# The head of a decoder layer: conditioning vector spread by dense matmuls, constant matmuls in between, first k tile as plain fp32 products

## The chip, the core and the metric

The kernel runs on one core of a Trainium2 chip. A core has a matrix engine (TensorE, PE in the profile, with its weight loads as PEld), a vector engine (VectorE, DVE), a scalar engine for activation functions (ScalarE, ACT), GpSimd (POOL) and SyncE (SP), which here only issues DMAs. Each engine works through its own queue in order; semaphores tie the queues together. PE writes to PSUM, from which DVE or ACT fetch the results. The metric is the device time of one execution in microseconds; lower is better.

## The reference

One sequence of 256 tokens, width 2048, goes through one conditioned decoder layer (retention and HGRN2 side by side, then a convolutional feed-forward part) and a last RMSNorm. What matters here is the very start:

```python
mod = jax.nn.silu(c) @ w_ada[l] + b_ada[l]
shift1, scale1, gate1, shift2, scale2, gate2 = jnp.split(mod, 6, axis=-1)
h = modulate(rms_norm(x, g_norm1[l]), shift1, scale1)   # rms_norm(x)*(1+scale1)+shift1
p = h @ w_in[l]
```

`c` is one vector of 2048; `w_ada` is 2048 x 12288, `w_in` 2048 x 12288. All inputs are float32.

## The kernel before

**Layout.** Activations of the first stage stand transposed: `xT` has the 2048 features in 16 k tiles of 128 partitions, 256 tokens along the free dimension. The weights of `h @ w_in` come in 12 groups of 512 columns (`ATT`), each in k tiles of 128 x 512.

**Products.** To keep fp32 accuracy at the rate of the narrower type fp32r, each weight tile is split: `wh` is the tile rounded to fp32r by ACT (`upper`, L167), `wl` the rest, by DVE (`rest`, L172). The activation is split in the same way into a tile `hT` (halves "hi" and "lo"). A product is then three matmuls: hi x wh, lo x wh, hi x wl (`mm_cols`, L212, L213, L216, for groups whose result stays transposed; `mm_rows`, L196, L197, L201, for the others). Without the split, a plain fp32 matmul is one call, which the profile shows as two records.

**Modulation.** `silu(c)` is spread over all partitions as `sc` (128 x 2049, the last column 1 for the bias). `ada_dot` (L420) loads a tile of the transposed `w_ada` in two pieces of 1024 and 1025 columns and has DVE multiply each by `sc` and sum (L426): one dot for each partition. `scale_shift` makes with two such tiles the columns of scale and shift for one k tile (ACT, L437 to L440); `modulated` applies them to x (ACT L350, L354, for k = 0 DVE L352; DVE L355).

**The start, in order.** `constants` (L243) fills the tile `ones`, loads c as two rows on ACT's queue, then `ident` and `gn1`, and spreads c by matmuls with one row of ones against a row of c (L264), into four tiles of PSUM. `norm_x` (L325) loads x in four quarters on SP's queue, squares them (the first on DVE, the others on ACT) and adds each down to 256 columns on DVE; ACT takes Silu of the spread c out of PSUM in between, then switches to the table of Sqrt. `token_rstd` (L295) sums the squares over partitions on PE (L303), takes the root (ACT) and the reciprocal (DVE, L313), and spreads it over partitions by two matmuls with `ident` (L317); `times` (L413) multiplies x by it.

`run` (L760) writes the order of k tiles 0 and 1 by hand: dots of k = 0, then the first 4 groups (`FIRST`) of products with k tile 0, then k tile 1. Two groups stand in two single tiles of PSUM each (`po`, four buffers), two in a double tile (`pg`, two buffers). Up to L827 (`self.ordered = False`) everything that goes through `pin` keeps the program's order on its engine; behind it, the order on ACT, DVE and PE is laid out by a scheduler when the program is built. There the dots of k tile 2 and on run in the background, paced by `pump`; `take` (L790) takes a finished group out of PSUM (ACT L794 for a first part, DVE L796 to add).

**Loads.** All weight tiles share 12 buffers `raw` on SP's queue; a load is issued when its buffer is free and an earlier load has landed.

```python
self.pin(self.nc.sync.dma_start(out=raw, in_=src))
```

Of the kernel before, what the change touches and what calls it, by code (L numbers as in the profile page):

```python
# [19 lines left out]
P = 128  # L20
# [35 lines left out]
class Kernel:  # L56
# [145 lines left out]

    def mm_cols(self, ps, items, first, last):
# [39 lines left out]
    def constants(self):  # L243
# [13 lines left out]
        rows = [self.blk([1, GW], name="crow") for _ in range(2)]  # L257
        for u, row in enumerate(rows):
            nc.scalar.dma_start(out=row, in_=a["c"][:, u * GW : (u + 1) * GW])
        self.small_loads(nc.scalar, ("ident", "gn1"))  # L260
        for u in range(4):
            at = slice(u * G, (u + 1) * G)
            ps = self.po()
            nc.tensor.matmul(ps, lhsT=self.ones[0:1, :], rhs=rows[u // 2][:, u % 2 * G : (u % 2 + 1) * G], start=True, stop=True)  # L264
            self.silu.append((self.sc[:, at], ps))
# [29 lines left out]
    def token_rstd(self, parts):  # L295


        nc = self.nc
        ps = self.po()[:, :NT]
        for i, z in enumerate(parts):  # L300
            for t in range(NT):

                nc.tensor.matmul(  # L303
                    ps[:, t : t + 1],
                    lhsT=z[:, t * P : (t + 1) * P],
                    rhs=self.ones[:, 0:1],
                    start=i == t == 0,
                    stop=i == len(parts) - 1,
                    skip_group_check=True,
                )  # L310
        q = self.small([P, NT], name="rq")
        nc.scalar.activation(q, ps, AF.Sqrt, bias=self.eps1, scale=1.0 / D)
        self.pin(nc.vector.reciprocal(q, q))  # L313

        ps = self.po()[:, :T]
        for t in range(NT):
            nc.tensor.matmul(ps[:, t * P : (t + 1) * P], lhsT=q[:, t : t + 1].to_broadcast([P, P]), rhs=self.ident, start=True, stop=True)  # L317
        return ps
# [6 lines left out]
    def norm_x(self):  # L325
# [4 lines left out]
        for i, x in enumerate(self.xT):  # L330
            z = self.blk([P, 4, T], name="sq")
            if i == 0:
                self.pin(nc.vector.tensor_tensor(z, x, x, ALU.mult))
            else:
                if i < 3:
                    self.pin(nc.scalar.activation(*self.silu.pop(0), AF.Silu))
                self.pin(nc.scalar.activation(z, x, AF.Square))
            self.pin(nc.vector.tensor_tensor(z[:, :2, :], z[:, :2, :], z[:, 2:, :], ALU.add))
            self.pin(nc.vector.tensor_tensor(z[:, 0, :], z[:, 0, :], z[:, 1, :], ALU.add))
            parts.append(z[:, 0, :])  # L340
        for part in self.silu:
            self.pin(nc.scalar.activation(*part, AF.Silu))
# [3 lines left out]
    def modulated(self, dst, x, k, sc, sh):  # L346
# [4 lines left out]
        if k == 0:  # L351
# [68 lines left out]
    def ada_dot(self, src):  # L420

        nc = self.nc
        part = self.small([P, 2], name="dot", bufs=6)
        for u, w in enumerate((GW, D + 1 - GW)):
            raw = self.load(src[:, u * GW : u * GW + w], 1, w)
            dot = self.pin(nc.vector.scalar_tensor_tensor(raw[:, 0, :], raw[:, 0, :], 1.0, self.sc[:, u * GW : u * GW + w], ALU.mult, ALU.mult, accum_out=part[:, u : u + 1]))  # L426
# [5 lines left out]
    def scale_shift(self, name, k, sc, sh, gn):  # L432
# [6 lines left out]
        part = yield from self.ada_dot(self.a[name][k, 1])  # L439
        self.pin(act(sh[:, kk], part[:, 0:1], AF.Identity, bias=part[:, 1:2]))  # L440

# [318 lines left out]
    def run(self):  # L760
# [15 lines left out]
        def ada1(k):  # L776
# [3 lines left out]
            yield from self.scale_shift("ada1", k, s1, t1, self.gn1)  # L780
            if k % 2 == 0:
                hT[k // 2] = self.blk([P, 2, 2 * T], F32R, name="hT")
            self.modulated(act(k), self.xT[k // 4][:, k % 4, :], k, s1, t1)
# [16 lines left out]
        for _ in range(3):  # L800
            next(ada[0])
        rx = self.token_rstd(parts)
        rx_sb = c.tile([P, T], F32, name="rx_sb")
        ps = [self.po2(), self.po2(), self.pg(), self.pg()][:FIRST]
        for k in range(2):
            for i in range(4 if k else 1):
                if k and i == 1:
                    self.times(k, 1, rx)
                next(ada[k])
            if k == 0:  # L810
                self.times(k, 1, rx)

            ahead = 2 * k
            uppers = [self.upper(a["wa"][g][:, k : k + 1, :], 1, G) for g in range(ahead + 1)]
            rests = [self.rest(z) for z in uppers[:ahead]]
            for _ in ada[k]:
                pass
            for g in range(FIRST):
                if g >= ahead:
                    rests.append(self.rest(uppers[g] if g < len(uppers) else self.upper(a["wa"][g][:, k : k + 1, :], 1, G)))  # L820
                wh, wl = rests[g]
                if k == g == 0:
                    self.pin(nc.scalar.activation(rx_sb, rx, AF.Copy))
                mms[g](ps[g], [(act(k), wh[:, 0, :], wl[:, 0, :])], k == 0, k == 1 and g >= RESIDENT)
# [377 lines left out]
def _arrays(x, c, positions, w_ada, b_ada, g_norm1, w_in, w_ret_o, w_hg_o, w_out, hg_lb, g_norm2, w_up, conv_w, conv_b, w_down, g_final):  # L1202
# [4 lines left out]
        "c": c.reshape(1, D),  # L1207
# [45 lines left out]
```

## Time and profile before

| | us |
|---|---|
| median of 3 runs | 1513.63 (1513.56 to 1513.67) |
| the profiled execution | 1513.78 |
| its span, first to last instruction | 1512.0 |
| PE busy in the span | 1496.0 |
| DVE busy | 1206.4 |
| ACT busy | 846.6 |

Times in the rows of the timeline are counted from the start of the span: start, duration, engine, line of the kernel, operation, tiles (written from read), shape and count; in brackets stands how long the engine was idle before and what ended that. Rows of several instructions merge a run of like ones. PE's records end later than the next one starts, since matmuls are pipelined; the rate is read from starts. In the view of windows each row is a stretch: its length, then for PE, PEld, DVE, ACT and POOL the busy time with the number of instructions, PE's granted clock, the DMA share and GB/s. The column of the granted clock shows 1.00 for the whole head; that PE works at half rate there is seen in the spacing of its records alone.

### The profile page before, as it was taken

The numbers are of one execution on the slowest core, as the hardware profiler recorded it, in microseconds if no ns is written. First come the engines' busy times: TensorE is split into PE (matmuls) and PEld (weight loads), VectorE is DVE, ScalarE is ACT, GpSimd is POOL, SyncE is SP. The second block draws the span as 40 slices with busy tenths as digits, with TensorE's granted clock in tenths as the row PEclk, the third lists the DMA queues.
The fourth block names the chain that finished last, engine by engine and source line by source line (L and its number), as shares of the span: only waits on it lengthen the run. The fifth ranks groups of instructions, "written<-read, shape, count | busy, mean of one in ns | idle before, by whom it ended". The sixth has DMA issues, their size and how long they took to land.

```text
span 1512.0 us, 23190 instructions
## 1 busy us (share of the span) xinstructions
PE 1496.0 (99%) x8722; PEld 1288.2 (85%) x8722; DVE 1206.4 (80%) x1639; ACT 846.6 (56%) x1207; POOL 4.0 (0%) x8
## 2 busy tenths in 40 slices
PE   8999999999999999999999999999999999999997
PEld 6999999888888888888888888888888888888886
DVE  7899996997999877898977778778777769455794
ACT  6655454777875644455466555555655558344342
POOL 0000000000000000000000000000000000000000
PEclk9999999999999999999999999999999999999999
DMA  9999997777888889989847777777777766667651
GB/s 374 390 332 340 315 326 230 258 265 251 286 269 289 281 299 326 320 286 362 305 126 244 233 232 230 231 229 236 227 244 230 218 192 204 194 206 214 185 168 56
DMA packets 110996, 385.75 MB, mean 255 GB/s; under 512 B 12802, under 2 KB 13346, under 8 KB 110884
## 3 DMA queue, kind: packets, MB, share of 16 engines
q1 hardware_dynamic: 110016, 383.14, 76.8%
q8 instruction: 68, 1.11, 0.3%
q10 hardware_dynamic: 868, 1.13, 0.2%
q14 instruction: 44, 0.36, 0.1%
HBM read 382.11 MB, written 2.11 MB: 254 GB/s over the span
## 4 chain that ended last, share of the span: by engine, by line
PE 95%; DVE 3%; DMA 1%; ACT 1%; issue 0%; SPq 0%; DVEq 0%; ACTq 0%
PE pg L196 13%; PE pg L197 13%; PE pg L201 13%; PE po L1086 11%; PE pg L1086 10%; PE po L1088 5%; PE pg L1088 5%; PE po L201 3%; PE po L197 3%; PE po L196 3%; PE pg L212 3%; PE pg L213 3%; PE pg L216 3%; PE po L212 1%; PE po L213 1%; PE po L216 1%
## 5 line engine op out<-in xcount | busy, mean ns | idle before, releaser
L167 ACT ACTIVATE wh<-raw 128x1024 fp32r<-128x1024 f32 (+1 forms) x536 | 550.1, 1033 | 514.8 <-PE pg L197 181.1
L172 DVE TENSOR_TENSOR wl<-raw,wh 128x1024 fp32r<-128x1024 f32 (+1 forms) x536 | 634.0, 1189 | 236.0 <-ACT wh L167 232.7
L426 DVE SCALAR_TENSOR_TENSOR raw<-raw,sc 128x1024 f32<-128x1024 f32 x192 | 233.6, 1219 | 0.0
L1086 PE MATMUL po<-h2T,wh 128*128 128x512 f32 x704 | 221.1, 395 | 0.0
L1086 PE MATMUL pg<-h2T,wh 128*128 128x512 f32 x688 | 216.4, 396 | 0.0
L196 PE MATMUL pg<-wh,hT 128*128 128x512 f32 x512 | 202.8, 396 | 0.2 <-ACT p L794 0.2
L197 PE MATMUL pg<-wh,hT 128*128 128x512 f32 x512 | 200.0, 391 | 0.0
L1088 PEld LDWEIGHTS po<-h2T,wl 128*128 128x128 f32 x704 | 132.3, 188 | 31.2
L1088 PEld LDWEIGHTS pg<-h2T,wl 128*128 128x128 f32 x688 | 129.1, 188 | 31.1 <-DVE wl L172 0.5
L1088 PE MATMUL po<-h2T,wl 128*128 128x256 f32 x704 | 138.3, 278 | 0.0
L201 PE MATMUL pg<-wl,hT 128*128 128x512 f32 x512 | 137.4, 390 | 0.0
L1088 PE MATMUL pg<-h2T,wl 128*128 128x256 f32 x688 | 135.3, 278 | 0.1
L201 PEld LDWEIGHTS pg<-wl,hT 128*128 128x128 f32 x512 | 96.0, 188 | 20.4 <-DVE wl L172 0.2
L196 PEld LDWEIGHTS pg<-wh,hT 128*128 128x128 f32 x512 | 96.2, 188 | 19.9 <-ACT p L794 0.4
L197 PEld LDWEIGHTS pg<-wh,hT 128*128 128x128 f32 x512 | 96.2, 188 | 19.1
L1086 PEld LDWEIGHTS po<-h2T,wh 128*128 128x128 f32 x704 | 107.2, 189 | 0.0
L1086 PEld LDWEIGHTS pg<-h2T,wh 128*128 128x128 f32 x688 | 104.7, 189 | 0.0
L212 PE MATMUL pg<-hT,wh 128*128 128x256 f32 x384 | 95.2, 284 | 0.6 <-DVE p L796 0.6
L213 PE MATMUL pg<-hT,wh 128*128 128x256 f32 x384 | 95.1, 284 | 0.0
L212 PEld LDWEIGHTS pg<-hT,wh 128*128 128x128 f32 x384 | 74.1, 193 | 1.1 <-issue 0.8
L213 PEld LDWEIGHTS pg<-hT,wh 128*128 128x128 f32 x384 | 74.0, 193 | 0.3
L197 PE MATMUL pg<-wh,gs 128*128 128x512 f32 x176 | 68.6, 390 | 0.0
(250 smaller groups left out, 2062.7 us busy)
## 6 DMA issues: line engine op xcount, KB each, us to landing
raw<-in_wup SPq DMA_DIRECT2D x176, 512.0 KB, 4.4
raw<-in_wdown SPq DMA_DIRECT2D x88, 512.0 KB, 4.3
raw<-in_wa SPq DMA_DIRECT2D x80, 512.0 KB, 5.7
raw<-in_ada SPq DMA_DIRECT2D x64, 512.5 KB, 5.8
raw<-in_ada SPq DMA_DIRECT2D x64, 512.0 KB, 5.6
raw<-in_wab SPq DMA_DIRECT2D x64, 512.0 KB, 4.9
raw<-in_gate SPq DMA_DIRECT2D x32, 512.5 KB, 4.2
raw<-in_wb SPq DMA_DIRECT2D x32, 512.0 KB, 4.7
```

The source lines that it names most:

```text
L167: self.pin(self.nc.scalar.activation(wh, raw, AF.Copy))
L172: self.last = self.nc.vector.tensor_tensor(wl, raw, wh.bitcast(F32), ALU.subtract)
L196: nc.tensor.matmul(ps[t], lhsT=act[:, hi], rhs=wh, start=first and i == 0, stop=False)
L197: nc.tensor.matmul(ps[t], lhsT=act[:, lo], rhs=wh, start=False, stop=False)
L201: nc.tensor.matmul(ps[t], lhsT=act[:, hi], rhs=wl, start=False, stop=last and i == len(items) - 1)
L212: nc.tensor.matmul(outs[j], lhsT=wh[:, cs[j]], rhs=act[:, :T], start=opens, stop=False, skip_group_check=True)
L213: nc.tensor.matmul(outs[j], lhsT=wh[:, cs[j]], rhs=act[:, T:], start=False, stop=False, skip_group_check=True)
L216: nc.tensor.matmul(outs[j], lhsT=wl[:, cs[j]], rhs=act[:, :T], start=False, stop=last and i == len(items) - 1, skip_group_check=True)
L426: dot = self.pin(nc.vector.scalar_tensor_tensor(raw[:, 0, :], raw[:, 0, :], 1.0, self.sc[:, u * GW : u * GW + w], ALU.mult, ALU.mult, accu ...
L1086: self.pin(nc.tensor.matmul(ps[j + z], lhsT=wh[:, cs[z]], rhs=act, start=kt == 0, stop=False, skip_group_check=bool(begun)))
L1088: nc.tensor.matmul(ps[j + z][:, :T], lhsT=wl[:, cs[z]], rhs=act[:, :T], start=False, stop=kt == KT - 1, skip_group_check=bool(begun))
```

## The change

Four parts, all ahead of the steady products.

1. c is loaded as 128 x 16 columns instead of two rows, ACT takes Silu of it there, and PE spreads it by 16 fp32 matmuls of a column, broadcast to 128 x 128, against `ident`. The four tiles of PSUM are then copied to `sc`, two by ACT, two by DVE. The last quarter of x is squared half by ACT and half by DVE, and goes to the sums as two parts.
2. `idle(n)` issues n fp32 matmuls of `ones` by `ones` whose result nobody reads: 5 ahead of the spread, 4 behind the sums of squares, 8 behind the spread of the reciprocal. The matmuls of this stage are pinned to program order.
3. k tile 0 of the first four groups is computed as plain fp32 products of the raw weight tile and the unsplit h (`mm_plain`), opening the sums in PSUM; the split halves of h for k tile 0, which later groups need, are made behind the first group of k tile 1.
4. The second piece of the dots for the shift of k tiles 0 and 1 is cut in two (`fine`), with one more addition on ACT; loads of k tile 1's dots and of k tile 0's weights alternate on SP's queue.

```diff
+    def mm_plain(self, ps, w, h):
+
+        for j in range(4):
+            out = ps[j // 2][:, j % 2 * T : (j % 2 + 1) * T]
+            self.pin(self.nc.tensor.matmul(out, lhsT=w[:, j * P : (j + 1) * P], rhs=h, start=j % 2 == 0, stop=False, skip_group_check=True))
...
-        rows = [self.blk([1, GW], name="crow") for _ in range(2)]
-        for u, row in enumerate(rows):
-            nc.scalar.dma_start(out=row, in_=a["c"][:, u * GW : (u + 1) * GW])
-        self.small_loads(nc.scalar, ("ident", "gn1"))
+        self.small_loads(nc.scalar, ("c", "ident"))
+        self.pin(nc.scalar.activation(self.c, self.c, AF.Silu))
+        self.small_loads(nc.scalar, ("gn1",))
+        self.idle(5)
         for u in range(4):
-            at = slice(u * G, (u + 1) * G)
             ps = self.po()
-            nc.tensor.matmul(ps, lhsT=self.ones[0:1, :], rhs=rows[u // 2][:, u % 2 * G : (u % 2 + 1) * G], start=True, stop=True)
-            self.silu.append((self.sc[:, at], ps))
+            for i in range(4):
+                k = 4 * u + i
+                self.pin(nc.tensor.matmul(ps[:, i * P : (i + 1) * P], lhsT=self.c[:, k : k + 1].to_broadcast([P, P]), rhs=self.ident, start=True, stop=True))
+            self.silu.append((self.sc[:, u * G : (u + 1) * G], ps))
+
+    def idle(self, n):
+
+        ps = self.pg()[0]
+        for _ in range(n):
+            self.pin(self.nc.tensor.matmul(ps[:, :P], lhsT=self.ones, rhs=self.ones, start=True, stop=True))
...
+        self.idle(4)
+        yield 0.0
         q = self.small([P, NT], name="rq")
         nc.scalar.activation(q, ps, AF.Sqrt, bias=self.eps1, scale=1.0 / D)
         self.pin(nc.vector.reciprocal(q, q))
...
-            nc.tensor.matmul(ps[:, t * P : (t + 1) * P], lhsT=q[:, t : t + 1].to_broadcast([P, P]), rhs=self.ident, start=True, stop=True)
-        return ps
+            self.pin(nc.tensor.matmul(ps[:, t * P : (t + 1) * P], lhsT=q[:, t : t + 1].to_broadcast([P, P]), rhs=self.ident, start=True, stop=True))
+        self.idle(8)
+        yield ps
...
             if i == 0:
+                self.pin(nc.scalar.activation(*self.silu[0], AF.Copy))
                 self.pin(nc.vector.tensor_tensor(z, x, x, ALU.mult))
+            elif i < 3:
+                self.pin(nc.scalar.activation(z, x, AF.Square))
             else:
-                if i < 3:
-                    self.pin(nc.scalar.activation(*self.silu.pop(0), AF.Silu))
-                self.pin(nc.scalar.activation(z, x, AF.Square))
+                self.pin(nc.scalar.activation(z[:, :2, :], x[:, :2, :], AF.Square))
+                self.pin(nc.vector.tensor_tensor(z[:, 2:, :], x[:, 2:, :], x[:, 2:, :], ALU.mult))
             self.pin(nc.vector.tensor_tensor(z[:, :2, :], z[:, :2, :], z[:, 2:, :], ALU.add))
-            self.pin(nc.vector.tensor_tensor(z[:, 0, :], z[:, 0, :], z[:, 1, :], ALU.add))
+            if i < 3:
+                self.pin(nc.vector.tensor_tensor(z[:, 0, :], z[:, 0, :], z[:, 1, :], ALU.add))
+            else:
+                parts.append(z[:, 1, :])
+            if i in (1, 2):
+                self.pin(nc.vector.tensor_copy(*self.silu[i]))
             parts.append(z[:, 0, :])
-        for part in self.silu:
-            self.pin(nc.scalar.activation(*part, AF.Silu))
+        self.pin(nc.scalar.activation(*self.silu[3], AF.Copy))
...
-        part = yield from self.ada_dot(self.a[name][k, 1])
+        part = yield from self.ada_dot(self.a[name][k, 1], (0, GW, GW + G, D + 1) if fine else (0, GW, D + 1))
         self.pin(act(sh[:, kk], part[:, 0:1], AF.Identity, bias=part[:, 1:2]))
+        if fine:
+            self.pin(act(sh[:, kk], part[:, 2:3], AF.Identity, bias=sh[:, kk]))
...
+        rstd = self.token_rstd(parts)
+        next(rstd)
+        for _ in range(2):
+            next(ada[0])
+        rx = next(rstd)
         rx_sb = c.tile([P, T], F32, name="rx_sb")
+        next(ada[0])
+        self.times(0, 1, rx)
+        for _ in ada[0]:
+            pass
+        h0 = self.s1([P, T], name="h")
+        self.pin(nc.vector.tensor_scalar(h0, self.xT[0][:, 0, :], s1[:, 0:1], t1[:, 0:1], ALU.mult, ALU.add))
+        self.times(1, 1, rx)
         ps = [self.po2(), self.po2(), self.pg(), self.pg()][:FIRST]
...
+        raws = [self.load(a["wa"][0][:, 0:1, :], 1, G)]
+        for g in range(FIRST):
+            next(ada[1])
+            if g + 1 < FIRST:
+                raws.append(self.load(a["wa"][g + 1][:, 0:1, :], 1, G))
+            self.mm_plain(ps[g], raws[g][:, 0, :], h0)
+            if g == 0:
+                self.pin(nc.scalar.activation(rx_sb, rx, AF.Copy))
+        ahead = [self.upper(a["wa"][g][:, 1:2, :], 1, G) for g in range(1)]
+        for _ in ada[1]:
+            pass
+        for g in range(FIRST):
+            wh, wl = self.rest(ahead[g] if g < len(ahead) else self.upper(a["wa"][g][:, 1:2, :], 1, G))
+            mms[g](ps[g], [(act(1), wh[:, 0, :], wl[:, 0, :])], False, g >= RESIDENT)
+            if g == 0:
+                hi, lo = act(0)[:, :T], act(0)[:, T:]
+                self.pin(nc.scalar.activation(hi, h0, AF.Copy))
+                self.pin(nc.vector.tensor_tensor(lo, h0, hi.bitcast(F32), ALU.subtract))
...
-        "c": c.reshape(1, D),
+        "c": cols(c),
```

More of the change, by code (lines that the diff above doesn't have):

```diff
@@ L301, in token_rstd @@
             for t in range(NT):
[L303 to L309, printed above, removed]
-                )
+                self.pin(
+                    nc.tensor.matmul(
+                        ps[:, t : t + 1],
+                        lhsT=z[:, t * P : (t + 1) * P],
+                        rhs=self.ones[:, 0:1],
+                        start=i == t == 0,
+                        stop=i == len(parts) - 1,
+                        skip_group_check=True,
+                    )
+                )
+        self.idle(4)
+        yield 0.0
         q = self.small([P, NT], name="rq")
@@ L350, in modulated @@
         self.pin(act(dst[:, :T], x, AF.Identity, bias=sh[:, k : k + 1], scale=sc[:, k : k + 1]))
-        if k == 0:
+        if k == 1:
             self.pin(self.nc.vector.tensor_scalar(h, x, sc[:, k : k + 1], sh[:, k : k + 1], ALU.mult, ALU.add))
@@ L418, in times, with ada_dot @@
         return ins
-    def ada_dot(self, src):
+    def ada_dot(self, src, cuts=(0, GW, D + 1)):
         nc = self.nc
[L423 to L426, printed above, removed]
+        part = self.small([P, 3], name="dot", bufs=6)
+        for u, (at, to) in enumerate(zip(cuts, cuts[1:])):
+            raw = self.load(src[:, at:to], 1, to - at)
+            dot = self.pin(nc.vector.scalar_tensor_tensor(raw[:, 0, :], raw[:, 0, :], 1.0, self.sc[:, at:to], ALU.mult, ALU.mult, accum_out=part[:, u : u + 1]))
             if not self.ordered:
@@ L430, in ada_dot, with scale_shift @@
         return part
-    def scale_shift(self, name, k, sc, sh, gn):
+    def scale_shift(self, name, k, sc, sh, gn, fine=False):
         act = self.nc.scalar.activation
@@ L779, in ada1 @@
                 self.tc.add_manual_dep(ins.ins, self.last.ins.name, NOSYNC, reason="behind the weights traced ahead of it")
-            yield from self.scale_shift("ada1", k, s1, t1, self.gn1)
+            yield from self.scale_shift("ada1", k, s1, t1, self.gn1, fine=k < 2)
             if k % 2 == 0:
                 hT[k // 2] = self.blk([P, 2, 2 * T], F32R, name="hT")
+            if k == 0:
+                return
             self.modulated(act(k), self.xT[k // 4][:, k % 4, :], k, s1, t1)
@@ L799, in run @@
         ada = [ada1(k) for k in range(KT)]
-        for _ in range(3):
+        rstd = self.token_rstd(parts)
+        next(rstd)
+        for _ in range(2):
             next(ada[0])
-        rx = self.token_rstd(parts)
+        rx = next(rstd)
         rx_sb = c.tile([P, T], F32, name="rx_sb")
-        ps = [self.po2(), self.po2(), self.pg(), self.pg()][:FIRST]
[L805 to L824, printed above, removed]
```

## The prediction

> **What bounds the kernel now.** The page first: the span, the engines' busy time, the shares of the chain that ended last. The profiled execution took 1513.78 us, 1.8 us more than its span; the median of the runs shown is 1513.63 us, so 0.15 us lower.
>
> ```profile
> span 1512.0 us, 23190 instructions
> ...
> PE 1496.0 (99%) x8722; PEld 1288.2 (85%) x8722; DVE 1206.4 (80%) x1639; ACT 846.6 (56%) x1207; POOL 4.0 (0%) x8
> ...
> PE 95%; DVE 3%; DMA 1%; ACT 1%; issue 0%; SPq 0%; DVEq 0%; ACTq 0%
> ```
>
> PE sets the time. So I ask where PE is not full, with the view of windows:
>
> ```profile
> 0.00:16.97 16.97, 11.88 (x28) 6.88 (x28) 11.53 (x26) 10.41 (x17) 0.20 (x4) 1.00 0.90 336
> 16.97:32.56 15.59, 14.51 (x96) 13.89 (x96) 15.17 (x26) 8.70 (x17) 0.00 (x0) 1.00 1.03 406
> 32.56:280.00 247.44, 246.93 (x1758) 233.44 (x1758) 214.17 (x277) 141.66 (x198) 1.91 (x2) 1.00 0.91 318
> ```
>
> From 32.56 us PE is busy 246.93 of 247.44 us. Whatever moves the start of that stretch moves the end of the program by as much; the change can work only on the 32.6 us ahead of it. There the DMA share is 0.90 and then 1.03 (336 and 406 GB/s), and DVE is busy 15.17 of 15.59 us: data and DVE are short there, not PE. The chain of the head says the same:
>
> ```profile
> 2.13 6.48 DMA xT<-in_xT
> ...
> 8.64 1.07 ACT sq L337
> ...
> 10.88 3.55 DVE raw L426 x6
> ...
> 14.56 1.24 PE po L317 x4
> ```
>
> x lands, its last quarter is squared, then come three dots in 3.55 us, 1.18 us each. PE's clock is read from starts in the timeline:
>
> ```profile
> 2.26 7.16 PE L264 MATMUL po<-crow,ones 1*128 1x512 f32 x8 [2.26 <-DMA crow<-in_c]
> ...
> 18.88 1.05 PE L216 MATMUL po<-hT,wl 128*128 128x256 f32 x4
> ...
> 19.74 0.41 PE L212 MATMUL po<-hT,wh 128*128 128x256 f32 x1
> ...
> 22.41 0.64 PE L216 MATMUL pg<-hT,wl 128*128 128x256 f32 x4
> ...
> 22.88 0.28 PE L212 MATMUL pg<-hT,wh 128*128 128x256 f32 x1
> ...
> 466.37 1.02 PE L717 MATMUL po<-p,p 128*128 128x256 f32 x4
> 467.23 0.61 PE L719 MATMUL po<-p,p 128*128 128x128 f32 x4
> ```
>
> At 18.88 four matmuls of 256 columns take 0.86 us from start to start, 0.215 each; at 22.41 0.47 us, 0.12 each. So the clock doubled at about 22 us, 5 us after the first product; 7 us of matmuls with one row (L264) had not opened it. A plain fp32 record of 256 columns takes 0.215 at full clock (L717: 0.86 for four), and one call makes two records.
>
> **The change part by part.** Spread of c and the norm: what the removed and added operations cost.
>
> ```profile
> 1.56 0.39 ACTq L271 DMA_DIRECT2D ident<-in_ident  x1
> ...
> 4.33 0.60 ACT L336 ACTIVATE sc<-po 128x512 f32<-128x512 f32 x1 [0.59 <-PE po L264]
> ...
> 5.86 1.06 ACT L337 ACTIVATE sq<-xT 128x1024 f32<-128x1024 f32 x1 [0.93 <-DMA xT<-in_xT]
> ...
> 9.72 0.69 DVE L338 TENSOR_TENSOR sq<-sq 128x512 f32<-128x512 f32 x1
> ...
> 10.45 0.42 DVE L339 TENSOR_TENSOR sq<-sq 128x256 f32<-128x256 f32 x1
> ...
> 10.79 1.22 DVE L426 SCALAR_TENSOR_TENSOR raw<-raw,sc 128x1024 f32<-128x1024 f32 x1
> ```
>
> ```profile
> ident<-in_ident ACTq DMA_DIRECT2D x1, 64.0 KB, 4.5
> ```
>
> ```profile
> L410 DVE CAST h2T<-h x12: 285/289/295, 775.7 to 789.2; 128x256 fp32r<-128x256 f32 x12
> ```
>
> Before, the spread needed only the row of c (PE starts at 2.26). Now it needs `ident`, which landed at 1.56 + 4.5 = 6.1 us. It moves up by one place on ACT's queue, so it lands between 3.3 (where the five idle matmuls, ten records of about 0.21 from 1.0 us, end) and 6.0; I take 4.8, the row's 6.1 less one quarter of x (512 KB at 406 GB/s, 1.3 us), with which ACT's loads seem to take turns. ACT has a table load, then Silu of 128x16, ahead of that; c is the first load on the queue. At half clock a 128-column fp32 record takes two passes, as long as one pass of 256: 0.215. The first 512 columns are 4 calls, 8 records, 1.7 us, with 0.2 of drain done at 6.7. Now ACT's order counts: Copy (0.60) stands ahead of the first Square (1.06), which was at 5.86; it ends at 8.4 instead of 6.9.
>
> DVE follows, all in program order: add and add (0.69 + 0.42 + gaps = 1.15), copy of 512 columns from PSUM, 1.15, copy, half a square 0.70, one add 0.72. No row shows that copy: a cast of 256 takes 0.285, so 0.57 for 512, and an add of 512 takes 0.69; I take 0.6 (another 0.1 would cost 0.2 in all). Sum: 8.4 + 4.9 = 13.3 us for the first dot, which was at 10.79: **2.5 us later**. The balance of squares between ACT and DVE does not pay for two copies and the wait for the spread.
>
> From dots to the first product:
>
> ```profile
> 14.34 0.16 DVE L313 RECIPROCAL rq<-rq 128x2 f32<-128x2 f32 x1
> ...
> 15.76 0.29 ACT L440 ACTIVATE t<-dot 128x1 f32<-128x1 f32 x1
> 15.82 0.42 DVE L416 TENSOR_TENSOR xT<-xT,po 128x256 f32<-128x256 f32 x1
> ...
> 16.35 0.41 DVE L352 TENSOR_SCALAR h<-xT,s,t 128x256 f32<-128x256 f32 x1
> ...
> 16.98 0.80 PE L212 MATMUL po<-hT,wh 128*128 128x256 f32 x2 [1.20 <-ACT hT L350]
> ...
> 17.30 2.49 DVE L172 TENSOR_TENSOR wl<-raw,wh 128x512 fp32r<-128x512 f32 x4
> ```
>
> Two dots 2.4, reciprocal 0.16, a dot 1.2, `times` 0.44, two half dots 0.68 each (as an add of 512), ACT's last shift 0.3, h0 0.41: 13.3 + 6.35 = 19.65. First product at 19.7 instead of 16.98. The reciprocal needs Sqrt: Copy of the fourth quarter, a table load and Sqrt end near 15, under the second dot. The broadcast (L317) hides under the third dot and the idle(8) (16 records at 0.11, 1.8 us at full clock, 3.4 at half) under what follows; at half clock it would end at 20.3, 0.6 too late. The idle(4) lies in PE's wait for the reciprocal.
>
> Products of k=0: split, 4 groups of 12 matmuls, 48 x 0.12 = 5.76 us at full clock; plain, 16 calls x 2 x 0.215 = 6.9. From 19.7 they end at 26.6, if the clock is open. What goes is four ACT copies and four subtracts, 2.49 us of DVE in this stretch; two more instructions (the halves of act(0)) are moved behind k=1's first group, one each on ACT and DVE (0.4).
>
> ```profile
> 24.62 0.08 DVE L426 DVE_READ_ACCUMULATOR raw<-raw,sc 128x1 f32 x1
> ...
> 25.86 0.75 PE L212 MATMUL po<-hT,wh 128*128 128x256 f32 x4 [0.66 <-ACT hT L350]
> ```
>
> k=1: after h0, DVE has `times` 0.44, three dots 3.6, two half dots 1.36: 25.05, against 24.7 before. The data for the last of them are 7 MB into the stream, as before; at 406 GB/s they are in by about 23, so DVE is last, not DMA. From there to PE was 25.86 - 24.62 = 1.24 us: ready at 26.3. PE is free at 26.6, so PE now comes last, and the 0.66 us wait goes. 5.76 us more: 32.4, with the drain 32.55.
>
> ```profile
> 31.71 0.64 PE L216 MATMUL pg<-hT,wl 128*128 128x256 f32 x4
> ```
>
> Before, this ended at 31.71 + 0.64 = 32.35. **Sum: +0.2 us.** Loads: the same bytes; two pieces of the shifts are halved, two issues more on SP (some 0.35 us each, hidden: SP waits for landings). The plain products keep their four raw buffers until PE has read them, about 22 to 26.6 us, where DVE freed them by 20; eight loads are on the way then, about 6 us of data, which covers it.
>
> What follows stays in place only if ACT lets it:
>
> ```profile
> 30.77 1.22 DVE L172 TENSOR_TENSOR wl<-raw,wh 128x1024 fp32r<-128x1024 f32 x1
> 30.89 0.30 ACT L437 ACTIVATE s<-dot 128x1 f32<-128x1 f32 x1 [0.94 <-DVE raw L426]
> ...
> 31.51 1.01 ACT L794 ACTIVATE p<-pg 128x1024 f32<-128x1024 f32 x1
> ...
> 32.57 0.50 PE L196 MATMUL pg<-wh,hT 128*128 128x512 f32 x1 [0.22 <-ACT p L794]
> ...
> 34.52 1.08 PE L201 MATMUL pg<-wl,hT 128*128 128x512 f32 x4
> ```
>
> PE's next group waits for the eviction p, which stood behind the scale s of k=2, and that for a dot. DVE now ends that dot about 2 us later (25.8 h, 26.3 lo, then four wl, lo of k=0, `times`, two dots: 32.85 against 30.85). This part is not in program order (L827), so p may stand ahead of s in the new program; p then starts at 31 and costs nothing. The next wl ends at 34.1, and PE wants it 1.95 us after 32.6, at 34.55: just in time.
>
> A rule against the row: the Trainium skill, "TensorE: Matmul & The Clock Gate", Part 1, says that only the first 3.4 us or so of matmuls run at half clock, counted in time and not in instructions. Taken alone, it would have opened the clock during L264, and the change would have nothing to win; the row of L264 (7.16 us) and the 0.215 at 18.88 do not agree, so operand rows seem to count.
>
> **The rivals.** 0.2% of the time, 3.0 us, is about what a measurement of this kernel can tell from no change.
>
> *The eviction stays behind the scale.* s at 32.9, two scales 0.65, p 1.0: PE resumes at 34.6, +2.0: 1515.8. For it: that is the order of before. Against: p's group ends 1.9 us ahead of the dot now. Chance 0.22.
>
> *Slower: the clock is shut at the first product.* Place: between the spread and 19.7 PE has only the ten small sums of squares (L303) and 12 idle calls, with gaps up to 1.5 us. Price: idle(8) late by 0.6, and every us at half clock loses 0.5; 5 us, as after 16.98, lose 2.5. With the 0.2: +3.3, 1517.1; if the idle calls count towards those 5 us, +1.9. It is slower by over 3.0 us if the clock comes later than 4.5 us after the first product. For it: the clock of before stayed shut through 1.24 us of L317 and the waits about it. Against: 16 calls of 128 rows are 6.9 us of dense work, more than the 5 that opened it before. Chance 0.17.
>
> *The spread is early.* `ident` at 3.3, or the clock open within the spread, so that the first 512 columns are out 0.9 to 1.5 us sooner. Then the first Square is bound by x's second quarter, the first dot comes at 11.85, the first product at 18.2, k=1 at 25.1: -1.5, 1512.3. The rule of the Trainium skill quoted above would open the clock by about 5 us and give about -0.7. Chance 0.17.
>
> *The whole head gains over 3 us.* k=1 would have to start before 23.2, with its last shift dot done by 22; its data are in at about 23. Only a better order later on could add to -1.5. Chance 0.04.
>
> **How the numbers follow.** Forecast +0.2 us, chance 0.40: 1513.78 + 0.2 = 1514.0 us. Its own range is 1513 to 1515. The range that leaves out 2 in 10 goes from below the early spread (1512.3, less 0.7 for cheaper copies) to just over the shut clock: 1511.6 to 1517.3. Slower by over 0.2%: two thirds of the shut clock, 0.11, and 0.03 for a shut clock and a late eviction together or a worse order later. Faster: 0.04 and 0.02 for the like. Within: 0.80.
>
> **What would show it.** Right: first dot near 13.3, first product near 19.7 at 0.215 per record, k=1 at about 26.6 with no wait for hT, and a dense PE from about 32.6. Wrong: 0.43 per record at the first product (shut clock), p behind s on ACT, `ident` landed by 3.5, or a start of dense PE off by more than 3 us.

## The result, and the profile after

The kernel after the change takes 1517.29 us (median of 11 runs, 1516.98 to 1518.44), the kernel before 1513.67 us beside it (11 runs): a ratio of 1.0024, interval 1.0016 to 1.0031. It is **slower by 3.6 us, 0.24%**. The forecast was +0.2 us with a range of 1511.6 to 1517.3: the time lies at the very edge of the range, and the loss is over the 0.2% that the prediction took as the line between a change and none. The profiled execution took 1517.3 us, 3.5 us more than that of before.

In kernel.py of after, the lines have moved: the spread of c is L271, the constant matmuls L278, the sums of squares L317, the spread of the reciprocal L334, the plain products L207, split products L218, L219, L222, the dots L450, the evictions L822.

The page of after, the two rows that answer to the first fence of the prediction:

```profile
span 1515.5 us, 23278 instructions
...
PE 1498.3 (99%) x8768; PEld 1294.4 (85%) x8768; DVE 1205.9 (80%) x1642; ACT 843.1 (56%) x1203; POOL 4.0 (0%) x8
```

PE is busy 2.3 us more, and the span is 3.5 us longer: PE bounds the time as before, and the stretch in which it is full begins later. The timeline of after, from the loads to k tile 1 (start, duration, engine, line, operation):

```profile
1.17 0.46 ACTq L284 DMA_DIRECT2D ident<-in_ident  x1
...
4.93 0.22 ACT L264 ACTIVATE c<-c 128x16 f32<-128x16 f32 x1 [1.99 <-DMA c<-in_c]
...
6.53 5.85 PE L271 MATMUL po<-ident,c 128*128 128x128 f32 x32 [2.97 <-DMA ident<-in_ident]
...
8.61 0.60 ACT L351 ACTIVATE sc<-po 128x512 f32<-128x512 f32 x1 [3.46 <-PE po L271]
9.11 1.99 ACT L354 ACTIVATE sq<-xT 128x1024 f32<-128x1024 f32 x2
...
14.92 1.22 DVE L450 SCALAR_TENSOR_TENSOR raw<-raw,sc 128x1024 f32<-128x1024 f32 x1
...
18.41 3.21 PE L278 MATMUL pg<-ones 128*128 128x128 f32 x16
...
20.72 0.41 DVE L839 TENSOR_SCALAR h<-xT,s,t 128x256 f32<-128x256 f32 x1 [0.42 <-ACT t L466]
...
21.45 3.62 PE L207 MATMUL po<-h,raw 128*128 128x256 f32 x16
24.91 3.62 PE L207 MATMUL pg<-h,raw 128*128 128x256 f32 x16
28.17 0.58 PE L218 MATMUL po<-hT,wh 128*128 128x256 f32 x2
```

PE waits 2.97 us for `ident` and starts the spread at 6.53. ACT's Copy stands ahead of its first Square and waits for the spread, so the Squares run from 9.11 (before: 5.86) and the first dot from 14.92 (before: 10.79). The first product is at 21.45 (before: 16.98). From there on the change works: the plain products take 6.72 us at full clock, and k tile 1 starts at 28.17 with no wait, where before it had waited 0.66 us at 25.86. So of the 4.5 us by which the first product is late, 2.3 are left at k tile 1. The chain of waits of after names the same path:

```profile
1.17 5.22 DMA ident<-in_ident
...
8.61 0.60 ACT sc L351
...
18.62 3.00 PE pg L278 x16
```

The clock in the head, by the view of windows (after the length of the stretch stands PE's busy time; the granted clock is the first of the last three columns; it shows a shut clock only after the clock had once been open):

```profile
14.00:18.00 4.00, 2.54 (x19) 2.38 (x20) 3.89 (x8) 1.41 (x5) 0.00 (x0) 0.95 1.03 389
18.00:22.00 4.00, 4.00 (x22) 3.95 (x22) 3.42 (x10) 1.02 (x4) 0.00 (x0) 0.62 1.04 403
```

The clock was shut again from about 17.6 us (0.95 of four us: 0.4 us at half rate) to 21.0 (0.62: 3.0 us at half rate), 3.4 us in all. The 16 records of the idle(8) fell into this stretch: they took 3.0 us, from 18.41 to the first product at 21.45. h had been ready at 20.72 + 0.41 = 21.13, so constant work held the first product for 0.3 us.

Behind k tile 1, the timeline of after with PE, ACT and DVE:

```profile
32.87 1.02 ACT L822 ACTIVATE p<-pg 128x1024 f32<-128x1024 f32 x1 [3.84 <-PE pg L222]
...
33.63 0.64 PE L222 MATMUL pg<-hT,wl 128*128 128x256 f32 x4
...
33.79 1.05 ACT L167 ACTIVATE wh<-raw 128x1024 fp32r<-128x1024 f32 x1
...
34.89 0.50 PE L196 MATMUL pg<-wh,hT 128*128 128x512 f32 x1 [0.62 <-ACT wh L167]
...
40.66 1.03 ACT L822 ACTIVATE p<-pg 128x1024 f32<-128x1024 f32 x1 [0.74 <-PE pg L201]
41.58 0.29 ACT L464 ACTIVATE t<-dot 128x1 f32<-128x1 f32 x1
...
43.03 1.22 DVE L450 SCALAR_TENSOR_TENSOR raw<-raw,sc 128x1024 f32<-128x1024 f32 x1
...
44.17 0.42 DVE L379 TENSOR_TENSOR hT<-h,hT 128x256 fp32r<-128x256 f32 x1
...
44.65 0.38 PE L219 MATMUL pg<-hT,wh 128*128 128x256 f32 x1 [1.03 <-DVE hT L379]
```

The rows of before that answer to wh, t and the low half of hT:

```profile
28.88 1.06 ACT L167 ACTIVATE wh<-raw 128x1024 fp32r<-128x1024 f32 x1 [2.06 <-DMA raw<-in_wa]
...
36.56 0.28 ACT L440 ACTIVATE t<-dot 128x1 f32<-128x1 f32 x1
...
40.72 0.42 DVE L355 TENSOR_TENSOR hT<-h,hT 128x256 fp32r<-128x256 f32 x1
```

Two things are new here. First, before, ACT made the split wh of the fifth group (the one that PE needs next) at 28.88, as soon as its data had landed and ahead of the eviction p. In after, the same data landed at 31.2, but ACT stands idle for 3.84 us, until 32.87, in front of the eviction, and wh is queued behind it: PE waits 0.62 us for wh and resumes at 34.89, 2.32 us later than before (32.57). Second, the shift t of k tile 2 now stands behind the eviction of the sixth group (before: of the fifth), 5.0 us later than before, and the low half of hT behind one more dot on DVE: PE waits 1.03 us at 44.65, where before it had no wait.

So the 3.5 us come in three steps. At 34.27, the end of k tile 1's products (before: 32.35), PE is 1.9 us late; the wait of 0.62 against 0.22 makes it 2.32; the wait at k tile 2 makes it 3.45. The same instructions of PE then stand 3.45 to 3.48 us later than before up to the end.

### The profile page after: what moved, and what is told of

It is laid out like the page before. It is cut to its first block, busy times and chain, and to the rows that moved or that the text cites. A ratio compares the mean times of both kernels' runs of the same rounds, so it can differ in the third digit from the quotient of the medians.

```text
span 1515.5 us, 23278 instructions
## 1 busy us (share of the span) xinstructions
PE 1498.3 (99%) x8768; PEld 1294.4 (85%) x8768; DVE 1205.9 (80%) x1642; ACT 843.1 (56%) x1203; POOL 4.0 (0%) x8
## 4 chain that ended last, share of the span: by engine, by line
PE 96%; DVE 2%; DMA 1%; ACT 0%; issue 0%; DVEq 0%; ACTq 0%
PE pg L196 14%; PE pg L197 13%; PE pg L201 13%; PE po L1121 11%; PE pg L1121 10%; PE po L1123 5%; PE pg L1123 5%; PE po L196 3%; PE po L197 3%; PE po L201 3%; PE pg L219 3%; PE pg L218 3%; PE pg L222 3%; PE po L222 1%; PE po L219 1%; PE po L218 1%
## 5 line engine op out<-in xcount | busy, mean ns | idle before, releaser
L450 DVE SCALAR_TENSOR_TENSOR raw<-raw,sc 128x1024 f32<-128x1024 f32 (+2 forms) x194 | 233.9, 1209 | 0.0
L219 PE MATMUL pg<-hT,wh 128*128 128x256 f32 x376 | 92.7, 283 | 1.0 <-DVE hT L379 1.0
L218 PE MATMUL pg<-hT,wh 128*128 128x256 f32 x376 | 92.8, 283 | 0.6 <-DVE p L824 0.6
L219 PEld LDWEIGHTS pg<-hT,wh 128*128 128x128 f32 x376 | 72.1, 192 | 1.4 <-DVE hT L379 1.2
L218 PEld LDWEIGHTS pg<-hT,wh 128*128 128x128 f32 x376 | 72.1, 192 | 1.1 <-issue 0.8
```

The costliest lines, as they stand in the source:

```text
L218: nc.tensor.matmul(outs[j], lhsT=wh[:, cs[j]], rhs=act[:, :T], start=opens, stop=False, skip_group_check=True)
L219: nc.tensor.matmul(outs[j], lhsT=wh[:, cs[j]], rhs=act[:, T:], start=False, stop=False, skip_group_check=True)
```

## The experiments

The theory behind them: the late spread (`ident` as a condition, Copy ahead of Square) costs the head about 3 us, and the order that the scheduler lays out for ACT and DVE behind the edited part costs another 1.5. Rivals: the constant matmuls hold PE up; the plain products hold their buffers, so that loads come late; the blocked SP queue delays the loads of the head. Part 4 of the change (the cut pieces and the alternating loads) stays in all of them and was not tried by itself. Each kernel is the one after, with the edit shown; its time stands beside runs of the kernel before on the same chip (medians 1513.80, 1513.81 and 1514.04 us in the three batches). All differences below are taken against these; after's own is +3.62 us.

### The three parts, one at a time

**The spread of c by rows, as before.** The old spread, the old Silu out of PSUM and the old squares (all four quarters whole); with the dense spread its idle(5) goes too. The idle(4), the idle(8), the plain products and the order of loads stay.

```diff
-        self.small_loads(nc.scalar, ("c", "ident"))
-        self.pin(nc.scalar.activation(self.c, self.c, AF.Silu))
-        self.small_loads(nc.scalar, ("gn1",))
-        self.idle(5)
+        rows = [self.blk([1, GW], name="crow") for _ in range(2)]
...
+            nc.tensor.matmul(ps, lhsT=self.ones[0:1, :], rhs=rows[u // 2][:, u % 2 * G : (u % 2 + 1) * G], start=True, stop=True)
...
+                    self.pin(nc.scalar.activation(*self.silu.pop(0), AF.Silu))
...
```

> The changed kernel with the old spread and the old squares: c as two rows, one-row matmuls, Silu out of PSUM, no five constant matmuls in front; the other constant matmuls, the plain products of k tile 0 and the new order stay. Theory A: first dot at 10.8, reciprocal at 13.3, first product at 17.2 to 17.7 at half clock, k tile 1 from about 25.5, dense PE from about 32.4, time near 1513.5, 3.5 us below the changed kernel. Theory B: dense PE stays behind 34, time over 1516.

Measured: 1514.48 us (1514.33 to 1514.78), +0.68, ratio 1.0004, interval 0.9994 to 1.0013. Its timeline:

```profile
10.73 1.22 DVE L443 SCALAR_TENSOR_TENSOR raw<-raw,sc 128x1024 f32<-128x1024 f32 x1
...
14.72 1.06 PE L333 MATMUL po<-ident,rq 128*128 128x128 f32 x4
...
15.82 0.42 DVE L433 TENSOR_TENSOR xT<-xT,po 128x256 f32<-128x256 f32 x1 [1.18 <-PE po L333]
...
18.36 3.72 PE L207 MATMUL po<-h,raw 128*128 128x256 f32 x16
...
31.90 0.50 PE L196 MATMUL pg<-wh,hT 128*128 128x512 f32 x1 [0.63 <-ACT wh L167]
...
41.67 0.38 PE L219 MATMUL pg<-hT,wh 128*128 128x256 f32 x1 [1.03 <-DVE hT L372]
```

The first dot is back at 10.73, and PE resumes at 31.90 instead of 34.89. The dense spread, with the copies and the divided squares that this run takes back together with it, costs 3.0 us in the trace and 2.9 in the medians. Both later waits (0.63 and 1.03) are still there, so they do not come from the late head: they belong to the order behind it. Spread and order together cost more than the 3.5 us of the loss, since the rest of the change wins: here PE resumes 0.67 us sooner than before (32.57) although it waits 0.4 us longer for wh, so that some 1.1 us are won ahead of it. And the idle(4) at half clock now holds the spread of the reciprocal: DVE waits 1.18 us for it.

**Split products for k tile 0 again.**

```diff
-            self.mm_plain(ps[g], raws[g][:, 0, :], h0)
...
+            mms[g](ps[g], [(act(0), wh[:, 0, :], wl[:, 0, :])], True, False)
```

> The changed kernel with k tile 0 of the first four groups as split products again. If the plain products pay: DVE has four subtracts and the low half (2.9 us) ahead of k tile 1's dots, k tile 1 starts at about 30.3 instead of 28.2, time 1519. If they cost (6.9 us of PE instead of 5.8): k tile 1 starts 1.1 us sooner, time 1516.2.

Measured: 1521.70 us (4 runs, 1519.59 to 1521.85), +7.9, ratio 1.0047, interval 1.0031 to 1.0062. The timeline shows the waits that the plain products had removed:

```profile
22.74 0.39 PE L218 MATMUL po<-hT,wh 128*128 128x256 f32 x1 [0.27 <-ACT wh L167]
...
30.95 0.50 PE L218 MATMUL po<-hT,wh 128*128 128x256 f32 x2 [1.51 <-ACT hT L374]
```

The first product is 1.3 us later than in after, mostly because the clock was shut for longer in this execution (the idle(8) ended at 22.5). k tile 1 waits 1.51 us for hT, since DVE has four subtracts between the dots; and with PE waiting, the clock was shut once more, from 32.4 to 35.8 us (records 0.21 us apart). PE resumes at 39.30, 4.4 us behind after. By the medians the plain products are worth 4.3 us within the change, by the fastest run of each 2.6: more than the roughly 2 us that I had put on them. How much of the 4.3 is the products' own is not shown: the longer shut clock ahead of the first product is in it, and the fastest run has no trace. The theory that they lose time falls.

**Without the constant matmuls.**

```diff
-        self.idle(5)
...
-        self.idle(4)
...
-        self.idle(8)
```

> The changed kernel without its 17 constant matmuls. If they keep the clock open, the first products run at 0.43 us per record for 3 us or more, and the time is 1518.5 to 1520. Theory C (they cost more than they bring: the clock shut at 17.6 us all the same, and the last eight run at half clock in front of the first product): first product 0.2 to 0.3 us sooner, and the time within 0.5 us of 1517.3 if the clock opens in the products as soon as with them.

Measured: 1519.34 us (5 runs, 1518.88 to 1519.7), +5.5, ratio 1.0036, interval 1.0023 to 1.0049. The timeline, for the first half of the plain products:

```profile
20.91 6.56 PE L207 MATMUL po<-h,raw 128*128 128x256 f32 x16 [2.57 <-DVE h L836]
```

and the view of windows:

```profile
26.00:30.00 4.00, 4.00 (x18) 3.43 (x18) 3.51 (x8) 2.71 (x6) 0.00 (x0) 0.91 0.94 328
```

The first product comes 0.54 us sooner (0.36 of that because `ident` landed sooner in this execution: the spread started at 6.17), but its 16 records take 6.4 us from start to start of the next group instead of 3.46: the clock was shut until 26.7 us (0.91 of the four us from 26: 0.7 us at half rate). The constant matmuls together are worth 1.9 us in the medians. They are not the loss.

### Why the head is late

**`c` and `ident` on SP's queue, ahead of x.**

```diff
-        self.small_loads(nc.scalar, ("c", "ident"))
+        self.small_loads(nc.sync, ("c", "ident"))
```

> The changed kernel with one edit: c and ident are loaded by SP's queue ahead of x, not by ACT's beside it. Theory A (late head: the spread waits for ident until 6.5 us, and the squares, copies and dots wait for the spread): ident lands by 3.5 to 4, first dot near 12.2 instead of 14.9, first product near 19 instead of 21.5, dense PE from about 32.5 instead of 34.9, and 1514 to 1515 us instead of 1517.3. Theory B (the end of the head is set behind the products: PE waits for the split of the next group, which ACT does behind an eviction): the head in front moves by 2.5 us, dense PE by under 1 us, time 1516.5 or more.

Measured: 1516.24 us (1515.91 to 1517.24), +2.4, ratio 1.0015, interval 1.0006 to 1.0025. Timeline:

```profile
3.52 4.75 PE L271 MATMUL po<-ident,c 128*128 128x128 f32 x32
...
12.88 1.22 DVE L450 SCALAR_TENSOR_TENSOR raw<-raw,sc 128x1024 f32<-128x1024 f32 x1
...
14.74 2.05 PE L278 MATMUL pg<-ones 128*128 128x128 f32 x8
16.59 1.06 PE L334 MATMUL po<-ident,rq 128*128 128x128 f32 x4
...
17.69 0.42 DVE L440 TENSOR_TENSOR xT<-xT,po 128x256 f32<-128x256 f32 x1 [1.18 <-PE po L334]
...
20.22 3.72 PE L207 MATMUL po<-h,raw 128*128 128x256 f32 x16
```

`ident` landed at 3.39 by the trace, and x paid for it: its first quarter landed at 5.52 instead of 4.73, and ACT waited for the others. So the spread starts 3.0 us sooner and the first dot 2.0, but the first product only 1.2. The clock opened early and was shut again by the time of the last sums: the idle(4) takes 2.05 us, the spread of the reciprocal starts at 16.59 although the reciprocal is done at about 15.4, and DVE waits 1.18 us for it, the same as with the spread by rows. So the late `ident` is a cause, and the idle(4) takes part of what an early `ident` gives. The wait of 0.62 us for wh and that at k tile 2 stayed.

**The same without the idle(4).**

```diff
-        self.idle(4)
```

> The first experiment (c and ident ahead of x, 1516.2) without the four constant matmuls behind the sums of squares. There they ran at half clock, 2.05 us, in front of the spread of the reciprocal, and DVE waited 1.2 us for it. Theory C (in a stretch where the clock is shut a constant matmul costs what it takes): that wait goes; the eight behind it, at half clock 3.4 us from 16.3, then hold the first product at 19.7 instead of 20.2; time 1515.7. If the four keep the clock, it opens one window (3.4 us) later without them and the time rises by up to 1.7 us.

Measured: 1515.56 us (1515.0 to 1516.49), +1.5, ratio 1.0010, interval 1.0000 to 1.0020: 0.9 us less than with it. The spread of the reciprocal is at 15.37 and the first product at 19.49. What is left of the loss is, by the trace, 0.36 us where PE resumes (32.93) and 1.15 at k tile 2.

**`gn1` loaded ahead of the Silu of c.** A load on ACT's queue that waits behind an activation landed at 11.59 us, and SP's queue waited 3.8 us for it.

```diff
-        self.small_loads(nc.scalar, ("c", "ident"))
+        self.small_loads(nc.scalar, ("c", "ident", "gn1"))
         self.pin(nc.scalar.activation(self.c, self.c, AF.Silu))
-        self.small_loads(nc.scalar, ("gn1",))
```

> The changed kernel with gn1 loaded ahead of Silu of c on ACT's queue. In the changed kernel SP's queue stood from 7.8 to 11.6 us for the landing of gn1, and the loads behind it land 1 to 2 us late. If data bind the head, k tile 1 and the next groups come up to 1 us sooner, 1516.3. By theories A and B (dots and order bind) the time stays within 0.3 us of 1517.3.

Measured: 1517.36 us (1517.16 to 1518.41), +3.3, ratio 1.0023, interval 1.0014 to 1.0033. `gn1` landed at 7.76, SP's wait for it fell from 3.8 to 1.0 us, and some loads landed up to 1.1 us sooner; the first product is at 21.30 instead of 21.45, and the time is that of after. In the head of after the loads on SP's queue do not bind; the rival falls.

### The order behind the head

**The split of the fifth group emitted first.** The generator's first step (which splits wh) is taken before the scheduler's part begins.

```diff
+        early = [next(self.pieces(a["wa"][FIRST][:, 0:2, :], 2))]
...
-                    take(g, self.products(mms[g], self.pg(), a["wa"][g], act, done[g], m), done[g] == 0)
+                    take(g, self.products(mms[g], self.pg(), a["wa"][g], act, done[g], m, steps=early), done[g] == 0)
```

> The changed kernel with one edit: the split of the first weight tile of the next group (fifth) is written ahead of the two evictions, in program order. Theory B: ACT does it at about 31.3, when its data land, PE resumes at 33.9 behind the eviction alone instead of 34.9, and the time falls by 0.9 us to 1516.4. Theory A: PE also resumes 0.9 us sooner, but that is all of it; the other 2.6 us stay. If the data bind (landing 31.2), nothing changes.

Measured: 1517.24 us (1517.04 to 1518.63), +3.4, ratio 1.0024, interval 1.0015 to 1.0034. The scheduler still put the eviction ahead of wh, and PE waited the same 0.62 us. The edit did not bring about what it was to test, so this says nothing of the order.

**The order written out by hand.** wh of the fifth group ahead of the evictions, and the rest of k tile 2's dots and halves ahead of the eviction of the sixth group, all pinned; the scheduler's part begins behind it.

```diff
-                    nc.scalar.activation(dst, z, AF.Copy)
+                    self.pin(nc.scalar.activation(dst, z, AF.Copy))
...
+        steps = begun(4, 2)
...
+        z = self.products(mms[4], self.pg(), a["wa"][4], act, 0, 2, steps=steps)
+        steps = begun(5, 2)
+        take(4, z, True)
...
+        six = begun(6, 3)
+        for _ in ada[2]:
+            pass
+        take(5, z, True)
```

> The changed kernel with the order of ACT and DVE written out by hand up to the sixth group: split of the fifth group's tile, evictions of groups three and four, scales of k tile 2, then the rest of k tile 2 ahead of the sixth group's eviction. Theory B (what is left behind the head is order): PE resumes at about 34.3 right behind k tile 1's last product instead of 34.9, the wait of 1.0 us for the low half of k tile 2 goes, together 1.7 us: 1515.6. If the data of these groups bind instead, the wait moves to the next tile and the time stays at 1517.3.

Measured: 1516.79 us (1515.78 to 1517.06), +3.0, ratio 1.0017, interval 1.0008 to 1.0026. ACT's timeline:

```profile
32.13 1.06 ACT L167 ACTIVATE wh<-raw 128x1024 fp32r<-128x1024 f32 x1 [2.16 <-DMA raw<-in_wa]
33.67 1.02 ACT L822 ACTIVATE p<-pg 128x1024 f32<-128x1024 f32 x1 [0.47 <-PE pg L222]
...
40.13 0.29 ACT L464 ACTIVATE t<-dot 128x1 f32<-128x1 f32 x1 [0.30 <-DVE raw L450]
40.45 0.60 ACT L374 ACTIVATE hT<-xT,t,s 128x256 fp32r<-128x256 f32 x1
...
41.45 1.00 ACT L822 ACTIVATE p<-pg 128x1024 f32<-128x1024 f32 x1
```

and further on, in the chain of waits:

```profile
136.43 0.96 ACT wh L167
137.43 0.39 PE pg L218
```

wh now runs while ACT had been idle, and t and hT ahead of the eviction. Both waits of PE are gone, so they were made by the order. PE is 2.3 us late at the start of the dense stretch and stays so past k tile 2. Two things eat into the gain. In this execution the clock was shut from 14.8 to 21.6, and the first product was at 22.22, 0.77 later than in after. And at 137 us a new wait for wh appears (0.46 us), behind which PE is 3.0 us late instead of 2.3.

**Spread by rows and the order by hand together.** The first and the last edit in one kernel.

```diff
+        rows = [self.blk([1, GW], name="crow") for _ in range(2)]
...
+        steps = begun(4, 2)
...
```

> The kernel with the old spread (the third experiment, 1514.5) with the same order by hand. If head and order add up: 1514.5 - 1.7 = 1512.8, 0.9 us below the kernel before. If PE meets its data instead, since the loads of the head run at the same 400 GB/s, it stays at 1513.7 or more.

Measured: 1513.76 us (1513.64 to 1514.45), -0.05, ratio 0.9999, interval 0.9991 to 1.0008. By the trace, PE is 0.6 to 0.75 us ahead of before up to 120 us, and level with it from 134 us on, where it waits for wh (0.46 us). With the two causes taken away together the whole loss is gone; what would have been a gain is given back at 134 us.

### What the parts could bring

**As the last, without the idle(4).**

```diff
-        self.idle(4)
```

> The same without the four constant matmuls behind the sums of squares, which ran at half clock (2 us) in front of the spread of the reciprocal there. The wait of 1.2 us for it ahead of the product with x goes; first product at 17.2 instead of 18.4, k tile 1 bound by its dots and data near 24.6 instead of 25.2: 0.5 us less than the kernel with them, 1512.3. If the clock then opens later, the products of k tile 0 lose up to 1.7 us and nothing is won.

Measured: **1512.90 us** (1512.63 to 1513.96), -0.9, ratio 0.9994, interval 0.9985 to 1.0003. Timeline:

```profile
13.88 1.22 PE L332 MATMUL po<-ident,rq 128*128 128x128 f32 x4 [0.55 <-DVE rq L328]
14.90 3.20 PE L277 MATMUL pg<-ones 128*128 128x128 f32 x16
17.94 3.62 PE L207 MATMUL po<-h,raw 128*128 128x256 f32 x16
```

The spread of the reciprocal now waits for nothing but the reciprocal. The first product is 0.97 us sooner than in the run with the idle(4) and runs at full clock all the same: the idle(4) was of no use. Only part of the 0.97 us is the idle(4)'s doing: the run by rows without the order by hand has the same head with the idle(4), and there the first product was at 18.36, 0.42 later than here. In the run just above, all 16 records of the idle(8) ran at half rate (3.4 us up to the first product; 2.8 in the run without the order by hand, 3.0 here). That the idle(4) costs something is said by the median, 0.86 us lower without it, and by the 0.9 us of the other pair of runs with and without it. Data are near here: DVE waits 0.34 and 0.65 us for pieces of `w_ada` ahead of k tile 1's dots. This is the best of all versions, 4.5 us better than after when each is set against its own runs of before, but its interval against before still holds 1.

**And without the idle(8).**

```diff
-        self.idle(8)
```

> The seventh experiment (1512.9) without the eight constant matmuls too, so with none at all. If they are what opens the clock at 17.5 us there: first product at about 17.4, at half clock for 3.4 to 6.8 us, k tile 1 1.2 to 2.5 us later, time 1514.1 to 1515.4. If the dense products open it as soon, time 1512.4.

Measured: 1514.37 us (1513.48 to 1514.9), +0.3, ratio 1.0001, interval 0.9992 to 1.0011. Timeline:

```profile
17.71 5.55 PE L207 MATMUL po<-h,raw 128*128 128x256 f32 x16 [2.57 <-DVE h L830]
```

The first product is 0.23 us sooner, but its group takes 5.4 us instead of 3.46. The idle(8) alone, in the 2.57 us in which PE waits for h, is worth 1.2 us between the medians.

## Why the prediction was wrong, by its steps

**Right: the path.** The prediction had the first Square behind the Copy, and the copies and the dots on one chain behind them, and so they are. From the start of the spread to the first dot it had 8.5 us (4.8 to 13.3); measured 8.4 (6.53 to 14.92). From there to the first product it had 6.35 (the terms that it lists add up to 6.27); measured 6.21 to the end of h, and 6.53 to the first product, which the idle(8) held up. For the plain products it had 6.9; measured 6.72. It had k tile 1 bound by PE, with the wait for hT gone, and the clock open at the first product; both are so. It took SP's added issues and the held buffers as free: in after PE waits for no load but `ident`, and moving `gn1` changed nothing.

**Wrong, first: the landing of `ident`.** The prediction had a row for it, 6.1 us, and took 1.3 off, because one place on ACT's queue seemed to be worth a quarter of x. It landed at 1.17 + 5.22 = 6.39, later than the row; even c, first on the queue, came at 4.9. One place on the queue gave nothing. By the landings in the trace, `ident` came 0.19 us behind the second quarter of x in both kernels (6.20 in after, 5.83 in before), and c 0.18 behind the first (4.73): c, now 128 x 16, had the turn beside the first quarter and left `ident` the second one. That turns are the reason is an argument, no run shows it. The spread began 1.7 us later than forecast, and all that follows with it: first dot +1.6, first product +1.75, end of k tile 1 at 34.27 instead of 32.55. This term makes up 1.7 of the 3.3 us between the forecast of +0.2 and the 3.5 of the profiled executions. An early spread needs `ident` ahead of x, as the run that loads it there shows (landed at 3.39).

**Wrong, second: ACT's order at the end of k tile 1.** The prediction weighed p ahead of the scale s (free) against p behind it (+2.0). p did come ahead of s, but ahead of wh too, for which PE waits next: +0.4 us (0.62 against 0.22). The order by hand removes it.

**Wrong, third: k tile 2.** The prediction ended its sum where the dense stretch begins and took everything behind as moved in step. The scheduler laid out another order there, and PE waits 1.03 us: +1.15. The same wait stands in the kernel with the spread by rows, where PE resumes 0.7 us sooner than before, and it is gone with the order by hand. So it comes from the order and not from the late head.

**The rival of the shut clock** came in part: the clock was shut from 17.6 to 21.0, so that the idle(8) ended late, but by 0.3 us and not 0.6, and the products themselves ran at full clock. The sum: 0.2 forecast, 1.7 for the late spread (with the 0.3 in it), 0.4, and 1.15, together 3.45 of the 3.5 us. That the time still touches the range is luck: its upper end was put there for a clock that is shut at the products, and they ran with it open.

**What stays open.** The wait for wh at 134 to 137 us in the kernels with the order by hand gives back 0.7 us. It lies in the scheduler's part; another order there was not tried. That the Copy stands ahead of the first Square is read from the trace; no run moved it by itself. Which part of the edit made the scheduler lay out another order is open too: both waits stand in the run without the dense spread, in the run without the plain products and in the run without the constant matmuls.

## What to carry to other kernels

Before a step is given a second condition (here a load of 64 KB for work that had needed a row of 4 KB), take the landing of that load from the trace as it stands. Here one place further up beside the stream of x won nothing, and a place ahead of the stream won 3 us and made x late by 0.8. In these runs constant matmuls paid (1.2 us) where PE waited right in front of dense products and nothing that it needed stood behind them; ahead of a short step on the critical path they cost (0.9 us). Where a scheduler lays out the rest, an edited head can change the order behind it, and a sum that ends where the edit ends misses that.

## What the runs showed of the hardware that was not expected

**The spread with 128 rows opened the clock, and a thin stretch shut it.** The 7.2 us of matmuls with one row in before had not opened it. The spread with 128 rows did. Whether the rows make the difference is not shown: the two spreads also differ in the columns of a record (512 and 128) and in the weight loads (PEld is busy 2.5 of 7.2 us in the old one and 5.7 of 5.9 in the new). The view of windows of after, its L271 records alone (each row: length, busy time with the records that touch it, clock, DMA):

```profile
6.50:8.65 2.15, 2.12 (x10) 1.00 1.05 377
8.65:10.80 2.15, 2.15 (x12) 1.00 0.99 349
10.80:12.40 1.60, 1.57 (x14) 1.00 1.02 402
```

A record of 128 columns takes 0.2 us up to 10.8 and about 0.11 behind it: the clock opened some 4.3 us after the start. It did not last: with PE busy 2.54 of the 4 us to 18.0, it was shut again at about 17.6. The shut stretches last 3.4 us in after, 6.8 with the order by hand and 10.2 without the constant matmuls (16.5 to 26.7): one, two and three times the same length. The Trainium skill, "TensorE: Matmul & The Clock Gate", Part 1, has the first 3.4 us or so at half clock and says that the window in which activity is watched runs freely, so that one kernel can meet it in different phases. The 4.3 us agree with that, as one such stretch and a part of the one before it.

**The phase shows in the times.** After was shut for 3.4 us in its profiled execution, the kernel with the order by hand for 6.8 (14.8 to 21.6), with the same head. The times of after lie in two groups, 8 runs from 1516.98 to 1517.56 and 3 from 1518.13 to 1518.44; those of the kernel with the order by hand too, 3 from 1515.78 to 1515.96 and 7 from 1516.72 to 1517.06. That the groups are the two phases fits, since the first products differed by 0.77 us. The mean granted clock of the runs points the same way: with the order by hand it was 0.997 to 0.998 in the 3 short runs and 0.996 in 5 of the 7 long ones (0.997 in two), in after 0.998 in 7 of the 8 short runs and 0.997 in the 3 long ones. Since only one execution of each has a trace, it is not shown.

**Small loads beside x land late.** In after, c (8 KB) was issued at 0.73 and used at 4.93; `gn1`, issued at 4.94, landed at 11.59, and where it was issued ahead of the Silu it landed at 7.76. With c and `ident` on SP's queue ahead of x, the spread started at 3.52.
